# The first of two gated networks takes the layout of the second, and the sums that feed its neighbours move to other places

## The chip, the cores and the metric

One core of a Trainium2 chip runs the whole program in one launch. The metric is device time in microseconds (us), and lower is better. The engines are TensorE (PE in the profile, with PEld for its weight loads), VectorE (DVE), ScalarE (ACT), GpSimd (POOL) and SyncE (SP), whose queue issues nearly all DMAs. Every engine works through its own queue in order, and the order of each queue is fixed when the program is built.

## The reference

A sequence of 512 tokens by 1024 channels passes four residual layers. Each is normed, scaled and shifted by numbers that come from one conditioning vector `c`, and added back through a gate from the same vector:

```python
def adaln_params(c, w, b):
    mod = jax.nn.silu(c) @ w + b
    shift, scale, gate = jnp.split(mod, 3, axis=-1)
...
def conv_ffn(h, w_up, conv_w, conv_b, w_down):
    up = h @ w_up
    a, b = jnp.split(up, 2, axis=-1)
...
    return (jax.nn.silu(a_conv) * b) @ w_down
...
    for i in range(DEPTH):
...
        hn = modulate(h, norm_g[i, 0], shift, scale)
        if i % N_MIXERS == 0:
            m = s5_mixer(...)
        else:
            m = fox_mixer(...)
        h = (h + gate * m).astype(x.dtype)
...
        f = conv_ffn(hn, ffn_w_up[i], ffn_conv_w[i], ffn_conv_b[i], ffn_w_down[i])
        h = (h + gate * f).astype(x.dtype)
    return rmsnorm(h, final_g)
```

So the layers are, by the kernel's index `i`: 0 the state-space mixer (s5), 1 the first gated network, 2 the forgetting attention (fox), 3 the second gated network. A network's inner width is 2816, which is 22 inner tiles of 128. `silu(c) @ w` is a product of one vector with a 1024x3072 matrix for each layer; its result has three thirds (shift, scale, gate), each of eight tiles of 128 numbers.

## The kernel before

Activations lie with channels on the 128 partitions and the 512 tokens along the free axis. All matmuls of weights run on fp32 numbers split into a high and a low part, three matmuls a product (high by high, high by low, low by high; `mms`, L294 to L298). A weight tile of 128x1024 arrives by DMA (`raw`, L189), ACT writes its high part (`w_hi`, L280), DVE the low part (`w_lo`, L281), and PE uses them at L297. `product` (L301) runs such products over a list of outputs; `add_residual` adds them to the residual `h` at L364.

**Stages in the order of time.** The mixer s5 (L1077) starts with the sums for its own norm and then loops over eight channel groups; its gated linear unit ("GLU") has four outputs prepared in the loop (L1198) and four more in a product, and evaluates `glu` (L1254) for all eight: a sigmoid on ACT, a product with `yt` read back from DRAM (DVE, L1257) and a split into `zhi` and `zlo`. `s5_w_out` follows. Then the first network (`ffn`, L583), the attention's values (`fox_values`, L1301), the forget gate's logarithm and cumulative sum (`log_forget`: `lf_ring` and `lf_out` on DVE, four small transposing matmuls at L1294, a scan at L1298 giving `nf_rows`, a trip through DRAM, `nfd` and `nf`, and a copy on POOL at L1408), the heads (`fox_qk`, with the softmax reduction at L1442), the attention's output product, the second network and the last norm.

**Two layouts of a network.** The first network (`plain=None`) has two groups of 11 inner tiles, `GROUPS`: all 11 are computed by `product` ("whole tiles": 2 outputs x 8 steps x 3 matmuls of 128x512 = 48 matmuls), then the group's product with `w_down` is run. The second (`plain=(0, 1, 2, 3)`) has four groups of 6, 5, 6 and 5 tiles, `QGROUPS`. Its inner tiles 0 to 3 are whole; the 18 others, 4 to 21, go through `quarters` (L515). A quarter tile takes the two outputs as a 2x2 matrix of blocks, and the activations likewise, and needs seven block products instead of eight: 7 x 4 steps x 3 matmuls of 128x256 = 84 matmuls (L552), with sums of weights (`sums`, L523) and of results on DVE. The sums of activations for it are made once, in `forms_x` (L476: `x` at L486, `sums` at L492). The products with `w_down` of a group lie between the tiles of the next one.

**The modulation sums.** There are two ways to compute a third of `silu(c) @ w`. `ada_pe` (L202) does it on PE, with the vector as the weights (L218), and turns the row into columns by small matmuls (L161, L166). `ada_units` (L242) does one tile of 128 numbers a step, a "unit": a DMA of 512 KB (`ada_raw`, L248) and one DVE reduction against a copy of `silu(c)` spread over the partitions (`ada_c`, from the DRAM row `c_row`; L249). Units are drawn by `tick` (L141) from a list `self.bg`; `done` draws what is left. Before, s5 does layer 0's three thirds and layer 1's first two on PE, and the first network draws 56 units: layer 1's gate, and all of layers 2 and 3.

**What sets the order.** Outside a few stretches written by hand, a scheduler orders each engine's queue when the program is built; it may take an instruction earlier than the code has it when its inputs are there by its own reckoning. Units depend only on their DMA and a buffer, so they move ahead easily. A helper's line stands for all who use it: L281 is every low part.

## Time and profile before

| | |
|---|---|
| three runs | median 1240.31 us (1239.1 to 1240.43) |
| the profiled execution | 1243.44 us, of which the span (first to last instruction) is 1241.4 us |
| granted TensorE clock | 0.99 of full |
| first network | 286 to 644 us |
| attention values | 644 to 692 us |
| second network | 890 to 1228 us |
| unit on DVE (L249) | 56 of them, 1.28 us each |

Times in views of the trace are microseconds from the span's start. A row of a timeline gives start, duration, engine, line, operation, output and inputs, the shape, and how many like it follow each other; in brackets stands how long the engine was idle before it and what ended that. Matmuls overlap in the pipeline, so the busy time of one is longer than the distance to the next; durations of matmul groups are read from the distance.

### The profile page before, as it was taken

The numbers are of one execution on the slowest core, as the hardware profiler recorded it, in microseconds if no ns is written. First come the engines' busy times: TensorE is split into PE (matmuls) and PEld (weight loads), VectorE is DVE, ScalarE is ACT, GpSimd is POOL, SyncE is SP. The second block draws the span as 40 slices with busy tenths as digits, with TensorE's granted clock in tenths as the row PEclk, the third lists the DMA queues.
The fourth block names the chain that finished last, engine by engine and source line by source line (L and its number), as shares of the span: only waits on it lengthen the run. The fifth ranks groups of instructions, "written<-read, shape, count | busy, mean of one in ns | idle before, by whom it ended". The sixth has DMA issues, their size and how long they took to land.

```text
span 1241.4 us, 19480 instructions
## 1 busy us (share of the span) xinstructions
PE 1213.7 (98%) x7506; PEld 1018.6 (82%) x7506; DVE 899.3 (72%) x1666; ACT 560.5 (45%) x1031; POOL 56.5 (5%) x109
## 2 busy tenths in 40 slices
PE   6999999999999999999999999999989999999997
...
DVE  6898796559887774443567467775799988888865
...
GB/s 268 253 275 222 202 196 266 129 100 204 292 267 236 256 248 111 102 75 77 139 69 102 129 142 128 104 130 21 118 52 111 107 117 89 118 105 104 102 86 68
DMA packets 74251, 183.75 MB, mean 148 GB/s; under 512 B 24135, under 2 KB 26527, under 8 KB 73135
## 3 DMA queue, kind: packets, MB, share of 16 engines
...
q10 hardware_dynamic: 288, 0.52, 0.1%
q14 instruction: 33, 0.27, 0.1%
...
## 4 chain that ended last, share of the span: by engine, by line
PE 83%; DMA 7%; DVE 5%; issue 2%; ACT 1%; POOL 0%; SPq 0%; DVEq 0%; POOLq 0%; ACTq 0%
PE mmp L297 47%; PE mmp L552 10%; DMA ada_raw<-in_ada_rows 5%; PE mmp L1169 5%; PE aux L552 4%; PE mmp L1334 3%; PE aux L973 2%; PE mmp L1198 2%; PE aux L1477 2%; PE mmp L218 1%; PE aux L1460 1%; DVE ada_raw L249 1%; PE aux L1062 1%; PE aux L1054 1%; DVE w_lo L281 1%
## 5 line engine op out<-in xcount | busy, mean ns | idle before, releaser
L280 ACT ACTIVATE w_hi<-raw 128x1024 fp32r<-128x1024 f32 (+4 forms) x197 | 181.2, 927 | 238.8 <-PE mmp L297 150.3
L281 DVE TENSOR_TENSOR w_lo<-raw,w_hi 128x1024 fp32r<-128x1024 f32 (+4 forms) x197 | 210.8, 1071 | 92.5 <-ACT w_hi L280 84.9
L297 PE MATMUL mmp<-a_hi,w_hi 128*128 128x512 f32 (+1 forms) x664 | 242.8, 367 | 2.0 <-ACT a_hi L434 1.3
L297 PE MATMUL mmp<-a_hi,w_lo 128*128 128x512 f32 (+1 forms) x664 | 240.0, 362 | 3.1 <-DVE w_lo L281 3.1
L297 PE MATMUL mmp<-a_lo,w_hi 128*128 128x512 f32 (+1 forms) x664 | 239.7, 362 | 0.0
L297 PE MATMUL mmp<-ghi,w_hi 128*128 128x512 f32 (+1 forms) x394 | 145.2, 369 | 2.1 <-ACT ghi L280 2.1
L297 PE MATMUL mmp<-glo,w_hi 128*128 128x512 f32 (+1 forms) x394 | 145.0, 368 | 0.1
L297 PE MATMUL mmp<-ghi,w_lo 128*128 128x512 f32 (+1 forms) x394 | 144.6, 367 | 0.0
L297 PEld LDWEIGHTS mmp<-a_hi,w_lo 128*128 128x128 f32 x664 | 125.5, 189 | 22.9 <-DVE w_lo L281 3.3
L297 PEld LDWEIGHTS mmp<-a_hi,w_hi 128*128 128x128 f32 x664 | 125.4, 189 | 22.6 <-issue 2.6
L297 PEld LDWEIGHTS mmp<-a_lo,w_hi 128*128 128x128 f32 x664 | 125.7, 189 | 17.5
L249 DVE CUSTOM_DVE_ANT_0 ada_raw<-ada_raw,ada_c,rest 128x1024 f32<-128x1024 f32 x56 | 71.7, 1282 | 29.0 <-DMA ada_raw<-in_ada_rows 28.9
L297 PEld LDWEIGHTS mmp<-ghi,w_hi 128*128 128x128 f32 x394 | 74.3, 189 | 14.3 <-ACT ghi L280 2.6
L297 PEld LDWEIGHTS mmp<-ghi,w_lo 128*128 128x128 f32 x394 | 74.4, 189 | 12.2
L297 PEld LDWEIGHTS mmp<-glo,w_hi 128*128 128x128 f32 x394 | 74.4, 189 | 12.1 <-DVE glo L281 0.5
L364 DVE SCALAR_TENSOR_TENSOR h<-mmp,par,h 128x512 f32<-128x512 f32 (+1 forms) x74 | 49.8, 676 | 42.9 <-PE mmp L297 42.9
L614 ACT ACTIVATE conv<-conv 128x512 f32<-128x512 f32 x44 | 27.6, 631 | 78.5 <-DVE conv L611 78.1
L552 PE MATMUL mmp<-w_lo,w_hi 128*128 128x256 f32 x216 | 59.7, 277 | 0.0
L552 PE MATMUL mmp<-w_hi,w_lo 128*128 128x256 f32 x216 | 59.7, 277 | 0.0
L552 PE MATMUL mmp<-w_hi 128*128 128x256 f32 x216 | 59.7, 277 | 0.0
L1169 PE MATMUL mmp<-a_x,raw 128*128 128x512 f32 x112 | 57.8, 655 | 0.0
L281 DVE TENSOR_TENSOR w_lo<-sums,w_hi 128x1024 fp32r<-128x1024 f32 x40 | 48.5, 1222 | 3.4 <-ACT w_hi L280 2.1
...
## 6 DMA issues: line engine op xcount, KB each, us to landing
...
```

The costliest lines, as they stand in the source:

```text
L249: nc.vector.tensor_tensor_reduce(w, w, self.crow, 1.0, self.ada_b[:, i, m:m + 1], ALU.mult, ALU.add, self.par[i][:, m:m + 1])
L280: nc.scalar.activation(hi, src, AF.Copy)
L281: nc.vector.tensor_tensor(lo, src, hi.bitcast(F32), ALU.subtract)
L297: self.last_mm = self.nc.tensor.matmul(o, wt, xt[:, cols], start=(k == 0 and n == 0), stop=(k == nk - 1 and n == 2),)
L364: self.nc.vector.scalar_tensor_tensor(self.h[:, m, cols], ps, self.par[i][:, 16 + m:17 + m], self.h[:, m, cols], op0=ALU.mult, op1=ALU.add,)
L552: self.last_mm = nc.tensor.matmul(o, wt[:, k], xt[:, k], start=(first and k == 0 and n == 0), stop=(k == H - 1 and n == 2), skip_group_che ...
L614: nc.scalar.activation(t, t, AF.Silu)
L973: nc.tensor.matmul(ps[g2][:, j, cols], x[rows, a + j, r].rearrange("p c j -> p (c j)"), self.rr[rows, planes, q, :], start=(j == 0 and r = ...
L1169: nc.tensor.matmul(ps, w[m][:, k, :], x[:, k], start=(k == 0), stop=(k == KT - 1))
L1198: nc.tensor.matmul(gps[m], wt, xt[:, k], start=(k == 0 and part == 0 and xt is yhi), stop=(k == KT - 1 and part == 1))
L1334: self.last_mm = nc.tensor.matmul(ps[q, b][:, :n], xt[:, k, tb], wt, start=(k == 0 and i == 0), stop=(k == KT - 1 and i == 2),)
L1477: nc.tensor.matmul(pv[:, c * P:], self.v[:, hp, k, r].rearrange("p t d -> p (t d)"), pp[:, r, c + 3 * k:NB + 3 * k, :].rearrange("p b t -> ...
```

## The change

- The first network is laid out like the second: four groups 6, 5, 6, 5, its down products between the tiles of the next group, its last down product with four outputs kept to the end (`tail=4` for 2). Whole are the inner tiles 0 to 3 and 6, 8, 10, 12, 14, 16, 18; the 11 others are quarter tiles (11 of the 18 tiles from 4 on).
- The first network draws 32 units and not 56: layer 1's gate and layer 2's three thirds, by a table `SUMS` over its tiles. The 24 units of layer 3 are drawn in the attention: four after each of the last two value groups, one after each output of `fox_qk`.
- Layer 0's gate third goes from PE to eight units, drawn in the GLU's product and ahead of `s5_w_out` (`ada_pool(pool, 4)`, `ticks=3`). The table of rows covers all four layers.
- `c_row` is written later: `sc` is transposed on PE, copied by ACT and stored as eight rows of 512 bytes, after the start of s5; before, it was one DMA of 1024 single numbers near the top of SP's queue.
- In the GLU the fifth output has its weights made ready earlier and its own PSUM, and its product runs ahead of the evaluation of the first four; `yt` has six buffers for two; `h` is loaded again later.

```diff
-GROUPS = (11, 11)
-ROWS_FROM = 1
-QGROUPS = (6, 5, 6, 5)
+ROWS_FROM = 0
+GROUPS = (6, 5, 6, 5)
 TAIL = 4
+WHOLE_TILES = (0, 1, 2, 3, 6, 8, 10, 12, 14, 16, 18), (0, 1, 2, 3)
+SUMS = (1, 1, 1, 1, 2, 2) + (2,) * 12
...
     def spread_c(self):
 
-        self.cd = self.dram.tile([1, D], F32, name="c_row")
-        self.nc.sync.dma_start(self.cd.rearrange("o (k p) -> p (o k)", p=P), self.sc)
+        nc = self.nc
+        self.cd = self.dram.tile([KT, P], F32, name="c_row")
+        ps = self.aux.tile([KT, P], F32, name="aux")
+        nc.tensor.transpose(ps, self.sc, self.ident)
+        rows = self.tmp.tile([P, S], F32, name="c_rows", tag="ssq", bufs=1)[:KT, :P]
+        nc.scalar.activation(rows, ps, AF.Copy)
+        nc.sync.dma_start(self.cd, rows)
...
-            for q, n in enumerate(groups):
-                fs = range(first[q], first[q + 1])
-                if not plain:
-                    up(fs, head=0 if q else 3)
-                    if q < last:
-                        down(q, range(KT))
-                    continue
-                for j, f in enumerate(fs):
+            for q, n in enumerate(GROUPS):
+                for j, f in enumerate(range(first[q], first[q + 1])):
                     if f == 0:
-                        up([0, 1], head=3, apart=True)
+                        up([0, 1], head=3)
                         todo.append(self.forms_x(pool, x, b))
-                    elif f in plain:
+                    elif f in whole:
...
+                    self.tick(sums[f] if f < len(sums) else 0)
+            self.done()
...
-            ada = [self.ada_pe(i, (2,), late=True), self.ada_pe(i + 1, (0, 1), late=True)]
...
-                    for _ in range((2, 2, 1, 1, 1, 1, 2, 2)[m]):
-                        next(ada[m >= 2])
-                    if m == 1:
-                        next(ada[0])
+                    next(ada)
...
-            for m in range(HEAD):
+            self.product(
+                self.io["s5_w_glu"], range(HEAD, HEAD + 1), KT, (yhi, ylo), lambda m, ps, cols: gps.update({m: ps}),
+                ready=ready,
+            )
+            for m in range(HEAD + 1):
                 glu(m, gps[m], slice(0, S))
-            self.product(self.io["s5_w_glu"], range(HEAD, KT), KT, (yhi, ylo), glu)
+            self.ada_pool(pool, 4)
+            self.bg = [self.ada_units(i, [2])]
+            self.product(self.io["s5_w_glu"], range(HEAD + 1, KT), KT, (yhi, ylo), glu, ticks=3)
+            self.load_x(resid)
+            self.done()
...
         lf = self.log_forget(ft, pool)
+        self.ada_pool(pool, 3)
         for q in range(2, NV):
             values((q,), range(NB), {q: load(q)})
+            self.tick(4)
...
-        self.product(self.io["fox_qk"], range(NH), KT, x, project, step=self.unit)
+        self.product(self.io["fox_qk"], range(NH), KT, x, project, ticks=1, step=self.unit)
+        self.done()
...
-        k.bg = [k.ada_units(1, [2])] + [k.ada_units(n, t) for n in (2, 3) for t in ([0, 1], [2])]
-        x = k.ffn(1, 0, x, k.norm_mod(2), ticks=1)
-        k.done()
+        k.bg = [k.ada_units(1, [2]), k.ada_units(2, [0, 1]), k.ada_units(2, [2])]
+        x = k.ffn(1, 0, x, k.norm_mod(2), WHOLE_TILES[0], SUMS)
...
+        k.bg = [k.ada_units(3, [0, 1]), k.ada_units(3, [2])]
         x = k.fox(2, x, k.norm_mod(3, HALF))
...
-        k.ffn(3, 1, x, k.norm_out(out), plain=(0, 1, 2, 3))
+        k.ffn(3, 1, x, k.norm_out(out), WHOLE_TILES[1])
```

After the change all lines stand some further down: L249 becomes L255, L281 becomes L287, L297 becomes L303, L1294 becomes L1302. Three places of the queues show what moved. The first is SP's queue at the very start of the program, before and then after (`first`, `rest`, `s_b` and the like are parameters of s5, `s_ud` is the first group's input on its way through DRAM):

```order
3 L108 DMA rest<-in_rest 128x416
4 L234 DMA c_row<-sc 128x8x1
5 L189 DMA raw<-in_ada_w 128x1024 x10
6 L189 DMA raw<-in_s_w_in 128x1024
7 L189 DMA raw<-in_ada_w 128x1024 x6
```

```order
9 L1143 DMA s_rr<-in_s_c 128x1024
10 L1144 DMA s_z<-s_zero 7x8x128
11 L967 DMA dd<-in_s_dd 128x128
12 L190 DMA raw<-in_s_w_in 128x1024
13 L240 DMA c_row<-c_rows 8x128
14 L1176 DMA s_ud<-uf 128x512
```

The store of `c_row` stood ahead of the first weights that layer 0's sums need, and now stands behind all of them. The second place is DVE's queue at the start of the GLU's evaluation, before and then after (`nm_t` holds the sigmoid, `ISA ada_raw` is a unit, and the `ISA par` row below it reads its sum out):

```order
329 L281 TENSOR_TENSOR w_lo<-raw,w_hi 128x1024
330 L1257 TENSOR_TENSOR nm_t<-nm_t,yt 128x8x64 x2
331 L281 TENSOR_TENSOR w_lo<-raw,w_hi 128x1024
332 L281 TENSOR_TENSOR zlo<-nm_t,zhi 128x512 x2
333 L281 TENSOR_TENSOR w_lo<-raw,w_hi 128x1024
334 L1257 TENSOR_TENSOR nm_t<-nm_t,yt 128x8x64 x2
```

```order
333 L255 ISA ada_raw,par_92<-ada_raw,ada_c,rest 128x1024
334 L255 ISA par_92 128x1
335 L1257 TENSOR_TENSOR nm_t<-nm_t,yt 128x8x64 x2
336 L255 ISA ada_raw,par_92<-ada_raw,ada_c,rest 128x1024
337 L255 ISA par_92 128x1
338 L287 TENSOR_TENSOR zlo<-nm_t,zhi 128x512 x2
339 L255 ISA ada_raw,par_92<-ada_raw,ada_c,rest 128x1024
340 L255 ISA par_92 128x1
341 L1257 TENSOR_TENSOR nm_t<-nm_t,yt 128x8x64 x2
```

All eight units stand between the eight evaluations, from row 333 to row 358; the last `zlo` is row 362. The third place is DVE's queue at the end of the attention's values, before and then after (`v` is a value block of the last group, `lf_out` the forget gate's logarithm, `nf_rows` its scan):

```order
787 L281 TENSOR_TENSOR v<-mmp,v 128x2x2x64
788 L730 SCALAR_TENSOR_TENSOR lf_ring<-lf_ring 128x64
789 L281 TENSOR_TENSOR w_lo<-raw,w_hi 128x1024
790 L730 SCALAR_TENSOR_TENSOR lf_ring<-lf_ring 128x64 x2
791 L730 SCALAR_TENSOR_TENSOR lf_out<-lf_ring 128x64
792 L281 TENSOR_TENSOR w_lo<-raw,w_hi 128x1024
793 L281 TENSOR_TENSOR v<-mmp,v 128x2x2x64 x4
794 L1298 SCALAR_TENSOR_TENSOR nf_rows<-lf_one,mmp 16x512
```

```order
921 L287 TENSOR_TENSOR v<-mmp,v 128x2x2x64
922 L732 SCALAR_TENSOR_TENSOR lf_ring<-lf_ring 128x64
923 L287 TENSOR_TENSOR w_lo<-raw,w_hi 128x1024
924 L732 SCALAR_TENSOR_TENSOR lf_ring<-lf_ring 128x64
925 L255 ISA ada_raw,par_95<-ada_raw,ada_c,rest 128x1024
926 L255 ISA par_95 128x1
927 L732 SCALAR_TENSOR_TENSOR lf_ring<-lf_ring 128x64
928 L255 ISA ada_raw,par_95<-ada_raw,ada_c,rest 128x1024
```

```order
931 L259 SCALAR_TENSOR_TENSOR ga_99<-par_95,rest 128x8
932 L255 ISA ada_raw,par_95<-ada_raw,ada_c,rest 128x1024
933 L255 ISA par_95 128x1
934 L732 SCALAR_TENSOR_TENSOR lf_ring<-lf_ring 128x64
935 L732 SCALAR_TENSOR_TENSOR lf_out<-lf_ring 128x64
936 L255 ISA ada_raw,par_95<-ada_raw,ada_c,rest 128x1024
937 L255 ISA par_95 128x1
938 L1306 SCALAR_TENSOR_TENSOR nf_rows<-lf_one,mmp 16x512
```

`lf_out` stood ahead of the last group's four `v`, and now stands behind them, behind one more `w_lo` and behind three units. All 24 units of layer 3 stand between row 829 and row 953, that is in the attention's norm, the values and the first head, not spread over the 16 outputs of `fox_qk`. On PE the four transposing matmuls that read `lf_out` stand in both kernels right behind the last value matmul and ahead of the first matmul of `fox_qk`. From the second head on, the queues of PE, DVE and ACT are in the same order in both kernels.

67 lines of the change are left out of this document (34 added, 33 removed).

## Prediction

> **What bounds the kernel now.** I read the page first: its busy times, its slices and the chain that ended last.
>
> ```profile
> PE 1213.7 (98%) x7506; PEld 1018.6 (82%) x7506; DVE 899.3 (72%) x1666; ACT 560.5 (45%) x1031; POOL 56.5 (5%) x109
> PE   6999999999999999999999999999989999999997
> DVE  6898796559887774443567467775799988888865
> PE 83%; DMA 7%; DVE 5%; issue 2%; ACT 1%; POOL 0%; SPq 0%; DVEq 0%; POOLq 0%; ACTq 0%
> ```
>
> PE is busy for 98% of the span, so matmuls that go are worth their time, wherever nothing else is late. DVE, at 72% on average, stands at eight or nine tenths at the start, around 370 us, and through the second network: there a microsecond given to DVE can come back as a wait of PE. So I went through the stages with a table of windows (duration; busy time of PE, PEld, DVE, ACT and POOL; granted clock; DMA share; GB/s).
>
> ```profile
> 70.00:170.00 100.00, 99.85 (x842) 65.09 (x842) 84.32 (x137) 47.06 (x149) 0.00 (x0) 0.98 0.73 230
> 206.45:228.30 21.85, 21.85 (x96) 18.08 (x97) 18.16 (x20) 12.46 (x19) 0.00 (x0) 1.00 0.70 226
> 405.00:410.00 5.00, 2.79 (x8) 1.62 (x7) 4.66 (x8) 3.35 (x5) 0.00 (x0) 0.79 0.73 220
> 644.00:692.00 48.00, 48.00 (x395) 47.68 (x395) 31.93 (x99) 18.45 (x35) 0.86 (x3) 1.00 0.27 88
> 692.00:708.00 16.00, 16.00 (x89) 13.13 (x88) 6.83 (x9) 5.81 (x8) 1.71 (x2) 1.00 0.50 164
> 898.00:938.00 40.00, 36.88 (x310) 36.68 (x309) 38.77 (x51) 22.53 (x30) 0.00 (x0) 0.96 0.19 67
> 940.00:1187.00 247.00, 247.00 (x1803) 232.33 (x1803) 213.51 (x316) 134.64 (x210) 0.00 (x0) 1.00 0.33 106
> ```
>
> In order: the loop of s5, the GLU's last four outputs, the group boundary of the first network, the attention's values, the first head, the start of the second network, and its quarter tiles. PE is full in all but the third and the sixth, where DVE is at its limit.
>
> **The change part by part: the first network.** The distance between matmuls is read from the chain where it follows PE without a wait.
>
> ```profile
> 945.65 4.08 PE mmp L552 x36
> 1072.46 6.81 PE mmp L297 x30
> ```
>
> A 128x512 matmul takes 6.81 / 30 = 0.227 us, a 128x256 one 4.08 / 36 = 0.1133. A whole tile is 48 x 0.227 = 10.90 us, a quarter tile 84 x 0.1133 = 9.52; eleven of them save 11 x 1.38 = 15.1 us. The down products keep their matmuls. Second, the boundary between the two groups of 11 goes: there PE waited for the last `ghi` of the group ahead of its down product, and in the new order another tile lies between.
>
> ```profile
> 407.71 0.64 PE L297 MATMUL mmp<-ghi,w_hi 128*128 128x512 f32 x1 [2.13 <-ACT ghi L280]
> 925.58 0.39 PE L297 MATMUL mmp<-a_hi,w_lo 128*128 128x256 f32 x1 [3.12 <-DVE w_lo L281]
> 924.31 1.22 DVE L281 TENSOR_TENSOR w_lo<-raw,w_hi 128x1024 fp32r<-128x1024 f32 x1
> ```
>
> The first row is 2.1 us of it; by the window PE is busy 2.79 of 5 us there, which is 2.2 us of idle time, and the clock of 0.79 costs about 0.21 x 5 = 1.05 more: 3.3 (2.2 to 4). In its place comes what the second network shows at its start: `forms_x` fills DVE (38.77 of 40 us), the `w_lo` of the next tile is late, and PE waits 3.1 us in one row, 40 - 36.88 = 3.1 in the window; the clock of 0.96 adds about 0.04 x 40 = 1.6, so 4.7. The first network will have the same instructions here, and one unit of 1.28 us more ahead of that `w_lo` on DVE: 6.0 us (3 to 8). Beyond it DVE has room on average: 213.51 / 247 = 86% in the quarter tiles of the second network, with 18 quarter tiles out of 18, against 11 of 18 here. But 32 units come on top.
>
> ```profile
> 281.68 1.28 DVE L249 CUSTOM_DVE_ANT_0 ada_raw<-ada_raw,ada_c,rest 128x1024 f32<-128x1024 f32 x1
> L249 DVE CUSTOM_DVE_ANT_0 ada_raw<-ada_raw,ada_c,rest 128x1024 f32<-128x1024 f32 x56 | 71.7, 1282 | 29.0 <-DMA ada_raw<-in_ada_rows 28.9
> ```
>
> They are 32 x 1.28 = 41 us in some 345, or 12%. The whole tiles between give room, so I take no further wait, and up to 6 us where units bunch. Sum: -15.1 - 3.3 + 6.0 = **-12.4 us** (-16 to -4).
>
> One rule speaks against this layout. The Trainium skill ("Perfetto Trace Analysis", "Identifying the Most-Contended Engine") holds matmul busy time a poor measure and has one judge TensorE by the busy share of its weight loads. By its measure the window of the second network is nearly at its end (232.33 of 247 us), and 84 loads for 48 are dear. The rival below prices this from rows.
>
> **The start.** The chain's longest pieces at the start, then the last sums on PE and what follows on DVE:
>
> ```profile
> 3.71 13.94 DMA c_row<-sc
> 17.66 10.54 DMA raw<-in_ada_w
> 28.24 1.05 PE L218 MATMUL mmp<-raw,sc 128*32 128x512 f32 x4 [0.24 <-DMA raw<-in_ada_w]
> 24.33 0.28 DVE L876 TENSOR_TENSOR s_pi<-s_w,s_w 128x64 f32<-128x64 f32 x1
> 31.43 0.17 DVE L171 SCALAR_TENSOR_TENSOR ga<-aux,rest 128x8 f32<-128x8 f32 x1 [6.82 <-PE aux L166]
> GB/s 0 35 131 289 397 363 381 371 375 288 143 37 33 20 61 111 180 283 283 115 262 438 397 426 426 401 442 397 401 422 418 397 401 422 418 393 406 418 397 406
> ```
>
> The store of `c_row`, 1024 writes of 4 bytes, takes 13.94 us. The last row is the transfer rate in 40 slices of 1 us: from about 9 to 20 us it falls from some 390 GB/s to as little as 20. Against 390 the twelve slices from 9 us on lack 4680 - 1816 = 2860 GB/s x us, or 7.3 us of transfer. Without the store the loads flow on, the last L218 comes some 7 us earlier, and `ga` is then held by DVE's own work, which ends at 24.61: 31.43 - 24.7 = **-6.7 us** (-4 to -7.3). The later store of eight 512-byte rows has nobody waiting until the GLU.
>
> **The loop of s5.** A fifth of the L218 instructions goes, 32 of 160 as the trace counts them, and ten small matmuls for the columns.
>
> ```profile
> L218 PE MATMUL mmp<-raw,sc x160: 589/593/1062, 18.3 to 174.9; 128*32 128x512 f32 x160
> 68.15 1.85 PE mmp L218 x16
> 30.36 1.03 PE L166 MATMUL aux<-sel,ada_rows 128*128 128x2 f32 x8
> ```
>
> That is 2 x 1.85 + 1.0 = 4.7 us of PE, in a loop where PE is busy 99.85 of 100 us and DVE 84.32. I take **-4.5** (-1, if DVE holds the pace at the loop's ends, to -4.7).
>
> **The GLU.** PE waited once ahead of the fifth output; its weights are now ready.
>
> ```profile
> 206.45 0.53 PE L297 MATMUL mmp<-a_hi,w_hi 128*128 128x512 f32 x1 [0.72 <-ACT nm_t L1256]
> 206.99 2.40 DVE L1257 TENSOR_TENSOR nm_t<-nm_t,yt 128x512 f32<-128x512 f32 x2
> 232.47 0.69 DVE L281 TENSOR_TENSOR zlo<-nm_t,zhi 128x512 fp32r<-128x512 f32 x1 [0.70 <-ACT zhi L280]
> ```
>
> That wait goes; the matmuls for the columns ahead of it only move forward. But DVE gets eight units among the eight evaluations. The last `zlo` ended at 232.47 + 0.69 = 233.2; PE wanted it for the eighth step of `s5_w_out`, at 228.3 + 21 x 0.227 = 233.1, just in time. After, DVE has from row 333 to row 362 eight units (10.2 us), eight L1257 (9.2 at 1.15 each, start to start 2.3 a pair), eight `zlo` (5.5 at 0.69) and four `w_lo` (4.6): 29.5 us from about 206 on, so 235.5. Whatever PE gains earlier it now waits for: 235.5 - 233.2 = **+2.3 us** (-1, if the evaluation starts earlier, to +6).
>
> **The attention.** The order puts `lf_out` behind the last values. The rows of before:
>
> ```profile
> 683.35 0.22 DVE L730 SCALAR_TENSOR_TENSOR lf_out<-lf_ring 128x64 f32<-128x64 f32 x1
> 691.45 1.50 DVE L281 TENSOR_TENSOR v<-mmp,v 128x256 fp32r<-128x256 f32 x4 [2.78 <-ACT v L280]
> 691.93 0.60 PE L1294 MATMUL mmp<-rest,lf_out 128*16 128x128 f32 x4
> 692.86 1.20 DVE L1298 TENSOR_TENSOR_SCAN nf_rows<-lf_one,mmp 16x512 f32<-16x512 f32 x1
> 698.10 8.05 DMA nf<-nfd
> 708.86 0.29 DVE L1442 CUSTOM_DVE_ANT_0 s<-aux,nf 128x128 f32<-128x128 f32 x1 [2.66 <-POOL nf L1408]
> ```
>
> `lf_out` was there 8 us before PE's transposing matmuls at 691.93. After, it waits for the `v` (1.5 us from 691.45), a `w_lo` (1.2), three units (3.8) and six short `lf_ring` (at most 0.22 each, 1.3): 699.2 at the earliest. Ahead of that, 14 units stand among the values and three in the norm, 21.8 us on top of 31.93 busy in a window of 48, 53.7 in all, so DVE arrives some 2 us late (0 to 6): 701.2. PE's queue holds those four matmuls ahead of all of `fox_qk`, and waits 701.2 - 691.9 = 9.3 us. From the scan on, `nf` took 16.0 us to the first reduction at 708.86, and PE's work on the first head filled them. Six more units lie in that stretch on DVE (7.7 us beside 6.83 busy of 16), and the transfers `nfd` and `nf` stand behind unit loads on SP: another 3 us (0 to 6). Sum **+12.3 us** (+7.3 to +16).
>
> Costed at nothing: the second network and the end, whose queues are the same; the whole norm ahead of the values, since PE has values to do while DVE takes three units.
>
> **The sum** against the profiled execution: -6.7 - 4.5 - 12.4 + 2.3 + 12.3 = -9.0, so 1243.4 - 9.0 = 1234.4 there. The median of the three runs is 3.1 us below that execution: 1240.3 - 9.0 = **1231.3 us**. What a measurement of this kernel can tell from no change is about 0.2%, 2.5 us.
>
> **The rivals.**
>
> *The unit loads starve the attention, slower.* What DVE waited for ahead of L249 (us, times):
>
> ```profile
>   DMA ada_raw<-in_ada_rows: 28.9, 29
> ```
>
> Half of the units of before waited for their DMA, 28.9 us in all. If the 14 units between norm and `lf_out` wait too, with PE behind `lf_out`, each wait adds in full: at 1 us each (28.9 / 29) it is 14 us, and the sum +5.0: 1245.3 us. It decides from 9.0 / 14 = 0.64 us a unit. For it: 24 x 0.5 MB in 60 us is 210 GB/s on top of the values' 88. Against: three buffers, and a rate of 390 to 440 at the start. 15%.
>
> *DVE keeps ahead everywhere, faster.* If `w_lo` and `zlo` stand ready when PE asks, no wait comes at `forms_x` (-18.4 for the network), the GLU gains 1, and the attention pays its least, 7.3: -6.7 - 4.5 - 18.4 - 1 + 7.3 = -23.3, 1217 us. Against: the second network does wait there. 13%.
>
> *The first network gains half.* Units bunched among quarter tiles cost 6 us more on DVE, which PE sees: 1231.3 + 6 = 1237.3 us. For it: the 86% of DVE in the quarter tiles. 11%.
>
> *Weight loads bound quarter tiles, much slower.*
>
> ```profile
> L297 PEld LDWEIGHTS mmp<-a_hi,w_hi 128*128 128x128 f32 x664 | 125.4, 189 | 22.6 <-issue 2.6
> ```
>
> At 189 ns a load, 84 loads are 15.9 us and 48 are 9.1, within the 10.90 of the matmuls; eleven tiles would cost 11 x 5.0 = +55 us in place of the 15.1 saved: 1231.3 + 15.1 + 55 = 1301 us. Against: 36 matmuls of L552, each with its load, take 4.08 us, so loads overlap. 1%. This is what the measure of the Trainium skill named above would make of it; the trace of the second network does not bear it out.
>
> **How the numbers follow.** The forecast, all terms within their bounds but not all at one end, has 60%, and spans about 1222 to 1240. The range must leave out at most 2 in 10: **1218 to 1244** leaves out half of each of the two outer rivals and the last. Faster by over 0.2%: 57 of the forecast's 60, 13 of the second, 5 of the third: 0.75. Slower: 13 of the first, 2 of the third, 1 of the last: 0.16. The rest, 0.09, is within 0.2%.
>
> **What would show it.** Start: `ga` near 25 us, no gap in the rate before 20. GLU: PE waits for `zlo` some 4 us into `s5_w_out`. First network: no wait of PE between the two halves, one of about 6 us for `w_lo` behind `forms_x`, and L552 at 0.113 us a matmul. Attention: a wait of PE of some 9 us ahead of the four transposing matmuls, ended by `lf_out`. I am wrong on the mechanism if that wait is absent, or if PE shows many small waits for `w_lo` among the quarter tiles.

## The result, and the profile after

| | before | after |
|---|---|---|
| median of 8 runs each, us | 1240.12 (1238.62 to 1247.93) | 1235.51 (1233.55 to 1238.12) |
| the profiled execution, us | 1243.44 (span 1241.4) | 1235.54 (span 1233.8) |
| granted TensorE clock | 0.990 | 0.987 |

The ratio of the times is 0.995, with a 95% interval of 0.9933 to 0.9967: faster by 0.5%. The forecast was 1231.3 us, with a range of 1218 to 1244.

From the page of the changed kernel: the busy times, the slices of PE and DVE, and the chain that ended last.

```profile
PE 1193.6 (97%) x8311; PEld 1042.2 (84%) x8311; DVE 987.3 (80%) x1824; ACT 597.2 (48%) x1102; POOL 57.0 (5%) x113
PE   7999998998999999999998899999989999999997
DVE  7898977669998986667789777765899888888865
PE 87%; DVE 7%; DMA 3%; ACT 1%; issue 1%; SPq 0%; POOL 0%; DVEq 0%; ACTq 0%; POOLq 0%
```

PE has 20 us less to do (1213.7 to 1193.6), and the span fell by 7.6. The difference has become waits. PE's row has new eights in slices 7, 10, 22 and 23 of 40; DVE's row has nines in slices 10 and 22. The waits of the changed kernel's PE, grouped by what ended them (us in total, times, longest), name them:

```profile
PE mmp L303 <- DVE w_lo L287: 11.4, 3, 4.8
PE mmp L1302 <- DVE lf_out L732: 8.4, 1, 8.4
```

Before, the same list had 3.1 us for `w_lo` and 2.1 for `ghi`, and nothing for `lf_out`. Three waits are new: in the GLU, at the start of the first network, and ahead of the four transposing matmuls. The third wait for `w_lo` is the second network's, which was there before.

**The start.** DVE's rows at the first norm, then the transfer rate of the first 40 us (one column a microsecond):

```profile
25.34 0.27 DVE L878 TENSOR_TENSOR s_pi<-s_w,s_w 128x64 f32<-128x64 f32 x1
25.48 0.16 DVE L172 SCALAR_TENSOR_TENSOR ga<-aux,rest 128x8 f32<-128x8 f32 x1
```

```profile
GB/s 0 27 182 344 309 270 322 381 412 424 410 414 406 406 393 422 414 406 401 356 340 385 430 418 418 422 401 418 401 418 418 393 397 422 399 396 299 41 12 8
```

The hole in the rate is gone, and `ga` follows DVE's own work without a wait, at 25.48 in place of 31.43.

**The GLU.** DVE's `w_lo` that PE waits for, PE's row at the wait, and the eighth evaluation and its `zlo` on DVE:

```profile
213.95 1.26 DVE L287 TENSOR_TENSOR w_lo<-raw,w_hi 128x1024 fp32r<-128x1024 f32 x1
215.27 0.79 PE L303 MATMUL mmp<-a_hi,w_lo 128*128 128x512 f32 x1 [3.48 <-DVE w_lo L287]
222.65 1.19 DVE L1257 TENSOR_TENSOR nm_t<-nm_t,yt 128x512 f32<-128x512 f32 x1 [2.27 <-ACT nm_t L1256]
224.88 0.69 DVE L287 TENSOR_TENSOR zlo<-nm_t,zhi 128x512 fp32r<-128x512 f32 x1
```

The last `zlo` is there at 225.6, and PE, which starts `s5_w_out` at 221.82, asks for it at 221.82 + 21 x 0.227 = 226.6: nobody waits for it. PE waits earlier, for a weight of the GLU's last output, which stands behind six of the units on DVE; and DVE's eighth evaluation then waits for that output (2.27 us).

**The first network.** The wait, what follows it, and a window of its steady part (duration; busy time of PE, PEld, DVE, ACT and POOL; clock; DMA share; GB/s):

```profile
308.80 0.58 PE L303 MATMUL mmp<-a_hi,w_lo 128*128 128x256 f32 x1 [4.78 <-DVE w_lo L287]
309.18 0.41 PE L303 MATMUL mmp<-a_hi,w_hi 128*128 128x256 f32 x1
309.39 0.41 PE L303 MATMUL mmp<-a_lo,w_hi 128*128 128x256 f32 x1
...
314.03 0.28 PE L303 MATMUL mmp<-a_hi,w_lo 128*128 128x256 f32 x1
314.15 0.28 PE L303 MATMUL mmp<-a_hi,w_hi 128*128 128x256 f32 x1
```

```profile
300.00:312.00 12.00, 7.22 (x51) 7.02 (x50) 12.00 (x13) 4.33 (x5) 0.00 (x0) 0.80 0.17 52
313.00:560.00 247.00, 247.00 (x1836) 233.71 (x1835) 202.69 (x295) 110.19 (x161) 0.12 (x1) 1.00 0.49 159
```

DVE is busy in all 12 us of the first window: it is not waiting for the weight. Ahead of that low part it has steps of `forms_x`, their low parts and the results of the tiles before to do; the last unit ahead of it starts at 284.19, the next one stands behind it (310.94). Past 313 us PE is never idle, though 11 of its tiles are quarter tiles with the units beside them. And the wait costs more than its length: until about 314 us the matmuls of 128x256 start 0.21 us apart, not 0.113.

**The attention.** PE and DVE at the transposing matmuls, then two windows on either side:

```profile
681.03 0.23 DVE L732 SCALAR_TENSOR_TENSOR lf_out<-lf_ring 128x64 f32<-128x64 f32 x1
681.40 1.01 PE L1302 MATMUL mmp<-rest,lf_out 128*16 128x128 f32 x4 [8.36 <-DVE lf_out L732]
```

```profile
624.00:673.00 49.00, 49.00 (x405) 48.73 (x403) 46.25 (x120) 20.02 (x39) 0.31 (x1) 1.00 0.60 208
673.00:701.00 28.00, 19.64 (x94) 15.66 (x94) 21.51 (x42) 5.78 (x8) 2.85 (x3) 0.82 0.82 283
```

In the first window, PE is full and DVE has 46.25 of 49 us; in the second PE has 19.64 of 28, at a clock of 0.82.

Where the time went, from the starts of the same instructions in both traces (us):

| up to | before | after | gained so far | this stretch |
|---|---|---|---|---|
| the 128x1 matmuls `aux<-par,raw` behind the first norm, L1150 | 44.70 | 38.47 | 6.2 | -6.2 |
| last prepared output of the GLU, L1198 | 203.0 | 192.8 | 10.2 | -4.0 |
| first matmul of `s5_w_out` | 228.41 | 221.82 | 6.6 | +3.6 |
| first matmul of the values | 644.04 | 624.76 | 19.3 | -12.7 |
| four transposing matmuls | 691.93 | 681.40 | 10.5 | +8.8 |
| first softmax reduction | 708.86 | 701.17 | 7.7 | +2.8 |
| end of the span | 1241.4 | 1233.8 | 7.6 | +0.1 |

### The profile page after: what moved, and what is told of

It reads as the page before. It is cut to its first block, busy times and chain, and to the rows that moved or that the text cites. A ratio compares the mean times of both kernels' runs of the same rounds, so it can differ in the third digit from the quotient of the medians.

```text
span 1233.8 us, 21319 instructions
## 1 busy us (share of the span) xinstructions
PE 1193.6 (97%) x8311; PEld 1042.2 (84%) x8311; DVE 987.3 (80%) x1824; ACT 597.2 (48%) x1102; POOL 57.0 (5%) x113
## 4 chain that ended last, share of the span: by engine, by line
PE 87%; DVE 7%; DMA 3%; ACT 1%; issue 1%; SPq 0%; POOL 0%; DVEq 0%; ACTq 0%; POOLq 0%
PE mmp L303 44%; PE mmp L558 16%; PE aux L558 6%; PE mmp L1171 4%; PE mmp L1342 2%; PE aux L975 2%; PE aux L1488 2%; PE aux L1471 1%; DVE w_lo L287 1%; PE aux L1064 1%; PE aux L1056 1%; PE mmp L219 1%; DMA ada_raw<-in_ada_rows 1%; PE aux L1441 1%; DVE ada_raw L255 1%
## 5 line engine op out<-in xcount | busy, mean ns | idle before, releaser
L287 DVE TENSOR_TENSOR w_lo<-raw,w_hi 128x1024 fp32r<-128x1024 f32 (+4 forms) x197 | 203.5, 1037 | 31.5 <-ACT w_hi L286 30.8
L303 PE MATMUL mmp<-a_hi,w_lo 128*128 128x256 f32 (+1 forms) x632 | 195.2, 310 | 11.5 <-DVE w_lo L287 11.4
L303 PE MATMUL mmp<-a_hi,w_hi 128*128 128x256 f32 (+1 forms) x632 | 197.9, 315 | 0.5 <-DVE conv L614 0.5
L303 PE MATMUL mmp<-a_lo,w_hi 128*128 128x256 f32 (+1 forms) x632 | 194.5, 308 | 0.0
L303 PE MATMUL mmp<-ghi,w_hi 128*128 128x512 f32 (+1 forms) x392 | 143.9, 367 | 0.0
L303 PE MATMUL mmp<-glo,w_hi 128*128 128x512 f32 (+1 forms) x392 | 143.9, 367 | 0.0
L303 PE MATMUL mmp<-ghi,w_lo 128*128 128x512 f32 (+1 forms) x392 | 143.6, 366 | 0.0
L303 PEld LDWEIGHTS mmp<-a_hi,w_lo 128*128 128x128 f32 x632 | 121.1, 192 | 19.3 <-DVE w_lo L287 12.7
L303 PEld LDWEIGHTS mmp<-a_hi,w_hi 128*128 128x128 f32 x632 | 121.3, 192 | 8.6 <-issue 2.6
L303 PEld LDWEIGHTS mmp<-a_lo,w_hi 128*128 128x128 f32 x632 | 121.4, 192 | 5.1
L286 ACT ACTIVATE w_hi<-sums 128x1024 fp32r<-128x1024 f32 x66 | 69.6, 1059 | 57.2 <-DVE sums L529 27.8
L558 PE MATMUL mmp<-w_hi 128*128 128x256 f32 x348 | 96.1, 276 | 0.0
L558 PE MATMUL mmp<-w_lo,w_hi 128*128 128x256 f32 x348 | 96.1, 276 | 0.0
L558 PE MATMUL mmp<-w_hi,w_lo 128*128 128x256 f32 x348 | 96.0, 276 | 0.0
L255 DVE CUSTOM_DVE_ANT_0 ada_raw<-ada_raw,ada_c,rest 128x1024 f32<-128x1024 f32 x64 | 81.7, 1283 | 12.6 <-DMA ada_raw<-in_ada_rows 12.4
L287 DVE TENSOR_TENSOR w_lo<-sums,w_hi 128x1024 fp32r<-128x1024 f32 x66 | 80.1, 1220 | 12.1 <-ACT w_hi L286 11.0
L370 DVE SCALAR_TENSOR_TENSOR h<-mmp,par,h 128x512 f32<-128x512 f32 (+1 forms) x92 | 62.1, 677 | 32.1 <-PE mmp L303 32.0
L303 PEld LDWEIGHTS mmp<-ghi,w_lo 128*128 128x128 f32 x392 | 73.6, 188 | 12.3
L303 PEld LDWEIGHTS mmp<-ghi,w_hi 128*128 128x128 f32 x392 | 73.6, 188 | 11.2
L303 PEld LDWEIGHTS mmp<-glo,w_hi 128*128 128x128 f32 x392 | 73.6, 188 | 11.1
L558 PEld LDWEIGHTS mmp<-w_lo,w_hi 128*128 128x128 f32 x348 | 65.3, 188 | 0.0
```

Source lines behind the costliest of these rows:

```text
L255: nc.vector.tensor_tensor_reduce(w, w, self.crow, 1.0, self.ada_b[:, i, m:m + 1], ALU.mult, ALU.add, self.par[i][:, m:m + 1])
L286: nc.scalar.activation(hi, src, AF.Copy)
L287: nc.vector.tensor_tensor(lo, src, hi.bitcast(F32), ALU.subtract)
L303: self.last_mm = self.nc.tensor.matmul(o, wt, xt[:, cols], start=(k == 0 and n == 0), stop=(k == nk - 1 and n == 2),)
L370: self.nc.vector.scalar_tensor_tensor(self.h[:, m, cols], ps, self.par[i][:, 16 + m:17 + m], self.h[:, m, cols], op0=ALU.mult, op1=ALU.add,)
L558: self.last_mm = nc.tensor.matmul(o, wt[:, k], xt[:, k], start=(first and k == 0 and n == 0), stop=(k == H - 1 and n == 2), skip_group_che ...
```

## The experiments

The theory is the prediction's: what PE gains is real, and part of it is given back where DVE's queue holds a unit ahead of something that PE wants. The rivals say that another cause limits each place: DVE's total work, the heads, the transfers, or the layout itself. Each of the twelve kernels starts from the changed one. Spans are those of one profiled execution each. Repeats of one kernel lie 2 to 8 us apart, the median of the kernel before was 1239.0 to 1241.8 us beside these runs, and the changed kernel was not run again beside them. So differences of a few microseconds are read from the stage that was edited. Most stages that an edit leaves alone repeat closely: from the first `s5_w_out` to the first value, the changed kernel, e1, e3, e5, e10 and e11 take 402.1 to 403.2 us. But from the first norm to the first `s5_w_out`, nine kernels that have no edit there take 181.5 to 185.5 us.

| kernel | median, us | ratio to before, 95% interval | span, us (after: 1233.8) |
|---|---|---|---|
| e1_fox_spread | 1230.67 | 0.991 (0.988 to 0.9939) | 1227.6 |
| e2_c_row_early | 1244.76 | 1.0019 (1.0001 to 1.0037) | 1245.1 |
| e3_glu_units_last | 1230.00 | 0.9906 (0.9875 to 0.9936) | 1229.3 |
| e4_eighteen_quarters | 1234.19 | 0.9945 (0.9925 to 0.9965) | 1232.8 |
| e5_fox_softmax | 1240.82 | 1.0011 (0.9994 to 1.0027) | 1237.0 |
| e6_ffn_units_later | 1233.08 | 0.9949 (0.9931 to 0.9966) | 1234.4 |
| e7_forms_later | 1248.36 | 1.0079 (1.0055 to 1.0104) | 1245.6 |
| e8_all_whole | 1243.59 | 1.0038 (1.0026 to 1.0049) | 1242.2 |
| e9_six_whole_first | 1227.16 | 0.9891 (0.9866 to 0.9916) | 1226.7 |
| e10_fox_thin | 1231.85 | 0.9935 (0.9916 to 0.9954) | 1232.1 |
| e11_fox_and_glu | 1224.52 | 0.987 (0.9851 to 0.9889) | 1222.7 |
| e12_all | 1217.95 | 0.982 (0.98 to 0.984) | 1216.2 |

Several kernels put units behind a named instruction of DVE. They share this edit: `unit_after` is an instruction that the scheduler must keep ahead of the units.

```diff
     def tick(self, n):
+        with self.behind(*([self.unit_after.ins] if self.unit_after else [])):
...
```

**1. The attention's units, spread over the heads (e1).** None is drawn between the value groups; two stand behind the low part of each of the first twelve outputs of `fox_qk`.

```diff
-            self.tick(4)
...
-                nc.vector.scalar_tensor_tensor(lo, ps, sc, hi.bitcast(F32), op0=ALU.mult, op1=ALU.subtract)
+                self.unit_after = nc.vector.scalar_tensor_tensor(lo, ps, sc, hi.bitcast(F32), op0=ALU.mult, op1=ALU.subtract)
...
-        self.product(self.io["fox_qk"], range(NH), KT, x, project, ticks=1, step=self.unit)
+        self.product(self.io["fox_qk"], range(NH), KT, x, project, ticks=2, step=self.unit)
```

> The changed kernel with one difference: the 24 units of layer 3 stand behind the low parts of the attention's first twelve outputs on DVE, two behind each, and none ahead of the forget gate. Theory A (PE's wait of 8.4 us for lf_out and the later arrival of nf come from the units' place on DVE): the wait goes, the first softmax reduction moves forward by about 11 us against the values' end, and the attention heads, where DVE is busy 95 of 143 us, take 31 us more without a wait: 1235.5 - 11 = 1224 us. Rival B (the units cost the same wherever they stand in the attention, since each head's chain from logits to weights is short of slack): the first wait goes, but each head grows by 1 to 1.5 us, 1232 to 1236 us.

The wait for `lf_out` is gone: from the first value matmul to the transposes 48.2 us, against 56.6 (and 47.9 before). From there to the first reduction it is 18.0 (19.8 after, 16.9 before). From the first reduction to the end 4.2 us come back (536.8, after 532.6), in part as a short wait at four of the pairs of heads:

```profile
PE aux L1444 <- DVE ot L1498: 1.2, 4, 0.4
```

So the wait was the units' doing. Of the 11.6 us that the attention lost, the span has 6.2 back, which lies between the two theories. The heads have some room for units, but not for 24, two at a time, at no cost.

**2. `c_row` early again (e2).** The store of 1024 single numbers goes back to the head of SP's queue.

```diff
-        ps = self.aux.tile([KT, P], F32, name="aux")
-        nc.tensor.transpose(ps, self.sc, self.ident)
...
-        nc.sync.dma_start(self.cd, rows)
+        self.nc.sync.dma_start(self.cd.rearrange("k p -> p k"), self.sc)
```

> The changed kernel with the store of c_row as it was before: 1024 writes of 4 bytes, ahead of the first weights on SP's queue. Theory A (that store holds up the loads behind it by some 7 us): ga comes at about 31.4 us instead of 25.5 and the whole span grows by 6.0 us, 1241.5 us. Rival B (the earlier ga came from the other edits at the start, or the loss is caught up in the loop, whose DVE is busy for 84 of 100 us): ga within 1 us of 25.5, or the span longer by less than 2 us.

The transfer rate of the first 40 us in this run, then two windows of the loop, and last the same windows of the changed kernel:

```profile
GB/s 0 38 152 383 317 328 365 393 366 312 98 8 45 33 74 176 246 184 168 246 381 397 422 410 430 410 426 406 418 393 422 406 418 393 418 410 422 377 418 418
```

```profile
38.00:60.00 22.00, 21.73 (x98) 12.05 (x95) 16.98 (x36) 12.76 (x29) 0.00 (x0) 0.84 0.59 203
120.00:160.00 40.00, 39.55 (x297) 25.34 (x296) 32.89 (x53) 17.70 (x52) 0.00 (x0) 0.96 0.52 152
```

```profile
38.00:60.00 22.00, 21.73 (x115) 12.08 (x115) 19.20 (x32) 13.38 (x38) 0.00 (x0) 0.92 0.62 193
120.00:160.00 40.00, 39.55 (x342) 25.46 (x341) 36.46 (x58) 19.31 (x59) 0.00 (x0) 1.00 0.48 135
```

The hole is back, and `ga` is late by 5.4 us (30.93), the matmuls `aux<-par,raw` by 5.7 (44.2). But the first `s5_w_out` is late by 9.7 and the span by 11.3. In the loop the granted clock is 0.84 and 0.96, as before the change, and not 0.92 and 1.00. The 0.96 from 120 to 160 us stands in these two kernels alone; the twelve with the later store have 1.00 there. From 38 to 60 us the clock differs with the store left late, too: 0.84 in e10, 0.92 in five kernels, 1.00 in six. So part of what the loop gained is the clock, and some of that hangs on the store; how the store reaches the clock 100 us later isn't settled. The theory had 6.0 us, so it was right on the place and short on the size. Form and place of the store were changed together, and which of the two counts wasn't run apart. This one store is worth all that the change gains: with it early the kernel is no faster than the one before.

**3. The GLU's units behind its last output (e3).** All eight are drawn after the last `zlo`.

```diff
-            self.product(self.io["s5_w_glu"], range(HEAD + 1, KT), KT, (yhi, ylo), glu, ticks=3)
+            self.product(self.io["s5_w_glu"], range(HEAD + 1, KT), KT, (yhi, ylo), glu)
+            self.tick(8)
```

> The changed kernel with the eight units of layer 0's gate behind the last zlo on DVE, and none among the eight evaluations. Theory A (PE's wait of 3.6 us for the last w_lo of the gated unit is DVE work that the eight units push back): the wait goes, and the residual of the first output of s5_w_out, which then waits for its gate some 10 us, is covered by four PSUM buffers of 5.4 us each: 1235.5 - 3.6 = 1232 us. Rival B (the time is only moved, PE waits for PSUM or for the next w_lo in s5_w_out): within 1 us of 1235.5.

The list of PE's waits in this run:

```profile
PE mmp L1307 <- DVE lf_out L735: 8.3, 1, 8.3
PE mmp L306 <- DVE w_lo L290: 7.9, 2, 4.8
```

One of the three waits for `w_lo` is gone, and the first matmul of `s5_w_out` is at 215.89, 5.9 us earlier for a wait of 3.5 (0.3 of the 5.9 is there at the first norm already). The span is 4.5 shorter; 1.4 is lost later, in the attention, where kernels without an edit there differ by as much.

**4. Eighteen quarter tiles (e4).** `WHOLE_TILES[0]` is `(0, 1, 2, 3)`, as in the second network.

```diff
-WHOLE_TILES = (0, 1, 2, 3, 6, 8, 10, 12, 14, 16, 18), (0, 1, 2, 3)
+WHOLE_TILES = (0, 1, 2, 3), (0, 1, 2, 3)
```

> The changed kernel with all 18 inner tiles from 4 on of the first network as quarter tiles, as in the second network, so 7 whole tiles more become quarter tiles. Theory A (PE sets the pace there, and DVE has room): 7 x 1.38 = 9.7 us less, 1226 us. Rival B (DVE sets it): DVE is busy 249 of 312 us in that stretch and gets 7 x 5.5 = 38 us more, 287 of 302; with units and tiles bunched, PE waits for w_lo again and again, and half or all of it is lost: 1231 to 1238 us.

The steady window of this run:

```profile
313.00:560.00 247.00, 243.21 (x1782) 228.50 (x1782) 240.57 (x369) 129.76 (x205) 0.13 (x1) 1.00 0.50 162
```

DVE goes from 202.69 to 240.57 of 247 us, and PE has waits: seven more quarter tiles, 9.7 us of matmuls, shorten the stage by only 3.3. Beside the units, DVE is full at eighteen, as rival B had it. The choice of eleven leaves little on the table.

**5. The units beside the softmax (e5).** Three behind the last reciprocal of each of the eight pairs.

```diff
-                nc.vector.reciprocal(sm[:, 1], sm[:, 0])
+                rec = nc.vector.reciprocal(sm[:, 1], sm[:, 0])
...
+            self.unit_after = rec
+            self.tick(3)
```

> The changed kernel with the 24 units of layer 3 behind the softmax of the attention's eight pairs of heads on DVE, three behind each pair's last reciprocal, and none ahead of the forget gate. With two units behind each of twelve low parts the wait for lf_out went, but the heads from the first softmax to the end grew by 4.2 us. Theory A (that growth came from units standing ahead of a head's logits and softmax): the heads stay as long as in the changed kernel, 532.6 us from the first softmax to the end, and the span is 10 to 11 us shorter than the 1233.8 of the changed kernel, 1223. Rival B (31 us more of DVE in the heads cost PE 4 us wherever they stand): 537 us from the first softmax to the end, a span of 1227 to 1228.

A miss on both sides: the stretch to the first reduction is 16.1 us and the best of all, and 16 us are lost behind it (548.7 from there to the end, after 532.6), 15 of them in the heads. PE's longest wait in total (`plo` is the low part of the probabilities), then POOL's scaling of the probabilities and two units of one pair on DVE beside it:

```profile
PE aux L1476 <- DVE plo L290: 12.8, 7, 2.1
```

```profile
732.61 4.51 POOL L1464 TENSOR_SCALAR s<-s,sm 128x384 f32<-128x384 f32 x4 [0.34 <-PE aux L1476]
...
733.65 1.27 DVE L258 CUSTOM_DVE_ANT_0 ada_raw<-ada_raw,ada_c,rest 128x1024 f32<-128x1024 f32 x1
...
734.84 1.71 DVE L258 CUSTOM_DVE_ANT_0 ada_raw<-ada_raw,ada_c,rest 128x1024 f32<-128x1024 f32 x1
```

In the changed kernel the same four instructions of POOL:

```profile
742.06 2.66 POOL L1462 TENSOR_SCALAR s<-s,sm 128x384 f32<-128x384 f32 x4 [0.35 <-PE aux L1471]
```

2.66 us became 4.51, and a unit beside them 1.71 in place of 1.27. What PE waits for (`plo`) is behind both; what the units' place on DVE costs and what the slower instructions cost wasn't run apart. So the same 24 units cost 4 us in one place of the heads and 15 in another.

**6 and 7. The start of the first network.** e6 takes the units away from its first four tiles; e7 moves the steps of `forms_x` as well, two to four behind the last `glo` (the low part of the gate's product) of tiles 1, 2 and 3, in both networks.

```diff
-SUMS = (1, 1, 1, 1, 2, 2) + (2,) * 12
+SUMS = (0, 0, 0, 0, 4, 4) + (2,) * 12
```

```diff
-                        for _ in range(4):
-                            if todo and next(todo[0], True):
-                                todo.pop()
+                        for _ in range((0, 4, 2, 2)[f] if f < 4 else 0):
+                            with self.behind(self.last_glo.ins):
+                                if todo and next(todo[0], True):
+                                    todo.pop()
```

> The changed kernel with the units of the first network kept behind its fifth tile: none on DVE from its start to the low part of the gate product of tile 3; four each after tiles 4 and 5, two after each later one. Theory A (PE's wait of 4.9 us near 304 is DVE work in a row, three units of it, 3.8 us): the wait falls to about 1.2 us and the slow clock after it mostly goes, 5 us less for the span, 1229. Rival B (it is the sums of activations alone, as in the second network, whose wait is 3.3 us without any unit): the wait falls by at most 1.6 us, the span is about 1232.

> As the kernel with the first network's units kept behind its fifth tile, and in both networks the sums of activations for the quarter tiles behind the gate products of tiles 1, 2 and 3 on DVE (four, two and two steps). Theory A (the wait for w_lo at a network's start is a matter of order: the sums stand ahead of the next whole tile's low part): the waits near 304 and 914 go in both networks, about 5 us each with the slow clock after them: 7 to 10 us less than 1233.8 in the span, 1224 to 1227. Rival B (DVE is short in total there: it was busy 38.8 of 40 us): the wait moves to the first quarter tile and keeps 3 us or more in each network, the span not under 1229.

PE's wait in e6, then the waits of e7 at its first quarter tile:

```profile
306.65 0.58 PE L306 MATMUL mmp<-a_hi,w_lo 128*128 128x256 f32 x1 [3.10 <-DVE w_lo L290]
```

```profile
318.42 0.38 PE L561 MATMUL aux<-w_hi 128*128 128x256 f32 x1 [1.74 <-ACT w_hi L289]
319.93 0.38 PE L561 MATMUL aux<-w_lo,w_hi 128*128 128x256 f32 x1 [1.13 <-DVE w_lo L290]
324.04 0.39 PE L561 MATMUL mmp<-w_hi 128*128 128x256 f32 x1 [2.55 <-ACT w_hi L289]
```

In e6 the wait falls from 4.8 to 3.1, what the second network has without units. Three units fewer stand on DVE ahead of that `w_lo` (in the changed kernel at 274.99, 276.27 and 284.19), 3.8 us of work, but it comes only 2.2 us earlier (305.38, after 307.53). That is close to rival B. A new wait of 0.9 comes at 360 us, and the stage is 0.7 shorter in all, which is within its scatter. In e7 the wait is gone and comes back as several at the first quarter tile, 8 us more in the stage (411.0 for 402.9), and most of the other 4 of the span in the second network, whose steps were moved too. This order doesn't mend it. In the first tiles DVE has more to do than PE, but e10 below shows another order that does mend it in the second network.

**8. No quarter tiles (e8).** All 22 tiles whole, in the new four groups, and no `forms_x` in the first network.

```diff
-WHOLE_TILES = (0, 1, 2, 3, 6, 8, 10, 12, 14, 16, 18), (0, 1, 2, 3)
+WHOLE_TILES = tuple(range(22)), (0, 1, 2, 3)
...
+                        if len(whole) < 22:
+                            todo.append(self.forms_x(pool, x, b))
```

> The changed kernel with all 22 inner tiles of the first network whole, in the four groups, and without the sums of activations that only quarter tiles need. Theory A (a quarter tile saves 1.38 us of PE, and the layout costs one wait at its start): eleven tiles cost 15.1 us more, and the wait of 4.9 us with 2.5 us of slow clock behind it goes: 7.7 us more, a span of 1241.5. Rival B (the quarter tiles give most of their saving back in waits that were there before in another place): within 2 us of 1233.8.

From the first `s5_w_out` to the first value 410.9 us, against 402.9 with quarter tiles and 415.6 before the change. So of the 12.7 us that this stretch gained, 8.0 are the quarter tiles, with their wait paid, and 4.7 the four groups and the fewer units.

**9. Relief for the first tiles (e9).** If DVE is short of time in the first tiles, whole tiles and fewer units there should help where moving did not. The first six tiles are whole (eleven in all, as after); layer 1's eight gate units go into `s5_w_out`, behind its residuals; the first six tiles draw none; `forms_x` is spread two steps a tile behind `glo` of tiles 1 to 4.

```diff
-WHOLE_TILES = (0, 1, 2, 3, 6, 8, 10, 12, 14, 16, 18), (0, 1, 2, 3)
-SUMS = (1, 1, 1, 1, 2, 2) + (2,) * 12
+WHOLE_TILES = (0, 1, 2, 3, 4, 5, 8, 10, 12, 14, 16), (0, 1, 2, 3)
+SUMS = (0,) * 6 + (2,) * 12
...
-                        for _ in range(4):
+                        for _ in range(4 if not sums else 2 if f < 5 else 0):
```

> The changed kernel with the same eleven quarter tiles in the first network, but the first six tiles whole, the sums of activations two steps behind each of the gate products of tiles 1 to 4, and layer 1's eight gate units in s5_w_out instead of here. Theory A (DVE is short over the first four tiles of the network, so order alone cannot mend it, but two more whole tiles of 4.8 us of DVE for 10.9 of PE and fewer units can): the wait of 4.9 us and the slow clock of 2.5 us behind it go, 5 to 7 us less than 1233.8 in the span, 1227 to 1229. Rival B (the sums and the preparation of the first quarter tile take DVE for over 20 us in a row wherever they stand, and PE waits there, as it did at the first quarter tile when the sums alone were moved): a wait of 3 us or more ahead of the first quarter tile, 1231 or above.

24 us of the first tiles in the changed kernel, up into its wait, and the same stretch in this run, whose tiles begin 0.6 us earlier and which has no wait for `w_lo` there:

```profile
282.00:306.00 24.00, 21.51 (x188) 21.15 (x186) 23.95 (x33) 15.68 (x22) 0.00 (x0) 1.00 0.14 50
```

```profile
281.40:305.40 24.00, 23.49 (x207) 23.32 (x207) 19.12 (x27) 13.96 (x20) 0.00 (x0) 1.00 0.46 156
```

DVE is at 19.12 us and no longer at 23.95, and the stretch from the first `s5_w_out` to the first value takes 396.5 us, 6.4 less. That is close to what the wait of 4.8 cost with its slow clock (7.0, worked out below). The edit does four things at once: more whole tiles first, the gate units elsewhere, no units in these tiles, and another order of `forms_x`; which of them it takes wasn't run apart.

**10. One unit behind each output, eight at the end (e10).** As e1, but one unit behind each of the 16 low parts, and two behind each of the first four residuals of the attention's output product.

```diff
+            def residual(m, ps, cols):
+                self.unit_after = add(m, ps, cols)
...
-                self.add_residual(i), head=4, tail=2, after=after,
+                residual, head=4, tail=2, after=after, ticks=2,
```

> The changed kernel with layer 3's units spread more thinly: one behind the low part of each of the 16 outputs of fox_qk, and eight in the attention's output product, two behind each of its first four residuals. With two behind each of twelve low parts the span was 1227.6 and the time from the first softmax to the end 536.8 us; with three behind each softmax 548.7; in the changed kernel 532.6. Theory A (a single unit fits between two steps of a head, units in a row hold up what stands behind them on DVE): 533 to 534 us from the first softmax to the end, a span of 1223 to 1225. Rival B (each unit in the heads costs its share, 4.2 us for 24): 16 units cost 2.8 us and eight in the output product 1 us more, a span of 1227.

Neither theory holds: 539.4 us from the first reduction to the end. Its parts say more. The stretch to the first reduction is 17.1 us, and the heads run as after the change (148.2 us from the first reduction to their last `aux<-phi,v`, after 148.0, and 152.5 in e1). But the output product is a bad place: it ends 40.0 us behind the heads, after 29.9. PE's waits there, grouped, then DVE's queue:

```profile
PE mmp L306 <- DVE h L373: 6.4, 2, 3.3
```

```profile
852.24 1.27 DVE L258 CUSTOM_DVE_ANT_0 ada_raw<-ada_raw,ada_c,rest 128x1024 f32<-128x1024 f32 x1
...
854.14 1.28 DVE L258 CUSTOM_DVE_ANT_0 ada_raw<-ada_raw,ada_c,rest 128x1024 f32<-128x1024 f32 x1
...
855.36 0.75 DVE L373 SCALAR_TENSOR_TENSOR h<-mmp,par,h 128x512 f32<-128x512 f32 x1
```

A residual reads its result out of PSUM; behind two units it is late, and PE waits for the space. Two other things differ in this run. The first `s5_w_out` is 2.5 us later, where nothing was edited; the loop's clock of 0.84 from 38 to 60 us is most of it. And the second network's wait of 3.1 us is gone, because the scheduler put a `w_lo` ahead of a step of `forms_x`, 6 us earlier than it stands in the changed kernel. That row, then 43 us of the second network's start in the changed kernel and in this run:

```profile
910.77 1.22 DVE L290 TENSOR_TENSOR w_lo<-raw,w_hi 128x1024 fp32r<-128x1024 f32 x1
```

```profile
888.00:931.00 43.00, 39.87 (x333) 39.51 (x333) 40.96 (x56) 23.55 (x32) 0.00 (x0) 0.96 0.23 76
```

```profile
888.00:931.00 43.00, 43.00 (x380) 43.00 (x380) 42.34 (x59) 24.87 (x36) 0.00 (x0) 1.00 0.23 72
```

PE is never idle there, with no work taken away, and from the end of the output product to the end of the span it takes 351.2 us, after 354.8. So the order alone was worth 3.6 us in the second network. Whether it would be enough in the first one, with units beside it, wasn't run.

**11 and 12. Together.** e11 is e1 and e3. e12 is e3, the relief of e9 (with four gate units in `s5_w_out` and four behind tiles 1 and 2) and e10.

```diff
+SUMS = (0, 2, 2, 0, 0, 0) + (2,) * 12
...
+            self.gate = self.ada_units(i + 1, [2])
+
+            def residual(m, ps, cols):
+                ins = add(m, ps, cols)
+                if 2 <= m < 6:
+                    with self.behind(ins.ins):
+                        next(self.gate)
```

> The changed kernel with two of the earlier moves together: layer 3's units two behind each of twelve low parts of the attention, and layer 0's gate units behind the last zlo. Alone they gave spans of 1227.6 and 1229.3 against 1233.8. Theory A (two separate waits, hundreds of us apart): the gains add, 6.2 + 4.5 = 10.7, a span of 1223.1. Rival B (one of them is only passed on): 1226 or above.

> The changed kernel with the three moves together: layer 0's gate units behind the last zlo; the first network with six whole tiles first and the sums of activations spread, layer 1's gate units four in s5_w_out and four behind the gate products of tiles 1 and 2; layer 3's units one behind each low part of the attention and eight in its output product. If each keeps what it gives alone (4.5 us, 5 to 7 us, 8 to 10 us): a span of 1213 to 1217. Rival: DVE, now 20 us fuller in s5_w_out and at the first network's start, makes PE wait there, and the span is 1220 or above.

In e11 the gains add: it has a span 11.1 us shorter than the changed kernel's, where e1 and e3 alone have 6.2 and 4.5. e12 is 17.6 us shorter, and beats both kernels: 0.982 of the one before. Not all of that is its three moves: its second network has the better order of e10 and gives 3.7, and its output product takes 9.7 more. PE's slices on its page, then a window from the GLU to the end of the first network:

```profile
PE   7999999999999999999999999997999999999997
```

```profile
210.00:620.00 410.00, 408.70 (x2935) 381.95 (x2934) 339.51 (x540) 187.35 (x276) 1.14 (x7) 1.00 0.47 156
```

The eights of the changed kernel are gone from PE's row; what is left is the seven at slice 28, two waits for residuals in the output product, 6.7 us together. The places of e1 have none there, at their own price in the heads; that combination wasn't run.

## Why the prediction was right or wrong, point by point

| term | forecast | measured |
|---|---|---|
| start | -6.7 | -6.2 |
| loop of s5 | -4.5 | -4.0 |
| GLU | +2.3 | +3.6 |
| first network | -12.4 | -12.7 |
| attention | +12.3 | +11.6 |
| the rest | 0 | +0.1 |
| sum, on the profiled execution | -9.0 | -7.6 |

- **The start** was right, and e2 shows that the store is its cause. That it reaches into the loop wasn't foreseen.
- **The loop** came out near its number for partly another reason. Up to the first prepared output of the GLU the gain was 11.6 us (176.5 to 164.9), 5.4 of it beyond the start; 1.4 went again before the last one. The matmuls saved and the clock can't be told apart here, and unedited kernels differ by 4 us over this part and the GLU; that the number fits is in part luck.
- **The GLU** was right in sign and wrong in mechanism and size. The sum took DVE's 29.5 us there as one block that ends with the last `zlo`, and let PE wait for its end, in `s5_w_out`. But the eighth evaluation can't begin before PE's last product is done, and PE waited for that product's own weight, whose `w_lo` stands in the middle of the block behind six units. That step was counted into the block and not followed to its reader, and the wait for `zlo` that the prediction named as its sign is absent. The wait of 3.5 us with the slow clock behind it costs 5.6 to 5.9 by e3; without the units the GLU would have gained some 2.
- **The first network** was right in its parts, nearly. The boundary's wait went, `forms_x` with a unit ahead of `w_lo` made a wait of 4.8 us where 6.0 in all were forecast, and the slow clock behind it added 2.2 (24 matmuls of 128x256 take 4.9 us from 309.18, for 2.7 at 0.113): 7.0. That matches e8: 15.1 less 7.0 is 8.1, and its quarter tiles gave 8.0. The rest is 4.7 by e8, where the sum had 3.3 for the boundary: so the wait came out dearer than its term and the rest larger, and the two errors all but cancel. The sum put 1.3 us on the units ahead of that `w_lo`; by e6 they are worth 1.7. DVE is full over the first tiles, and by e9 less work there with another order frees PE. It is not shown that only the work counts: e7's order moved the wait, e10's order took it away in the second network. Past 313 us, up to 560, no unit made a wait.
- **Weight loads** did not bound the quarter tiles. The row of 313 to 560 us has PEld at 233.71 of 247 us and no idle PE, and by e8 eleven tiles of 84 loads are 8 us faster than eleven of 48. The Trainium skill ("Perfetto Trace Analysis", "Identifying the Most-Contended Engine") names that share, beside the rate of matmul work against the peak (MFU), as what tells how close TensorE is to its limit. Here a share of 0.95 did not mean that more loads a tile cost time; that loads would stand one behind another was the prediction's reading of the page, and its rival at 1%.
- **The attention** was the best of the mechanisms: PE waited 8.4 us for `lf_out` (forecast 9.3), and the stretch to the first reduction grew by 2.8 (forecast 3). The rival that the loads of the units would starve it is refuted for the most part: over the whole kernel DVE waited for them 12.4 us, less than before.

```profile
L255 DVE CUSTOM_DVE_ANT_0 ada_raw<-ada_raw,ada_c,rest 128x1024 f32<-128x1024 f32 x64 | 81.7, 1283 | 12.6 <-DMA ada_raw<-in_ada_rows 12.4
```

The last unit ahead of the first softmax reduction, on DVE:

```profile
699.96 1.28 DVE L255 CUSTOM_DVE_ANT_0 ada_raw<-ada_raw,ada_c,rest 128x1024 f32<-128x1024 f32 x1 [2.18 <-DMA ada_raw<-in_ada_rows]
```

Its wait of 2.18 is one of the 12.4. The unit ends at 701.2, where the reduction starts, though POOL had the first part of `nf` ready at some 698.7 (two additions, 2.54 us from 697.45): that is most of the 2.8.

- **The time itself** was 4.2 us above the forecast. 1.4 is the sum's error. The other 2.8 is the step from the execution to the median: the profiled execution of before lay 3.1 us above its median, and the forecast took the whole sum off the median; the profiled execution of after lies on its own. The medians differ by 4.6 us where the executions differ by 7.9. So some of what the term-by-term table counts as gained is the profiled execution's own slowness, and the traces don't show which part.
